# Second block's conditioning on one core: last layer's share moved into the first block's output, bias copies ahead of the latent attention, two recurrence weights on another queue

## The chip, the cores and the metric

The kernel runs on one core of a Trainium2 chip. The core has TensorE (PE, matrix products), VectorE (DVE), ScalarE (ACT), GpSimd (POOL) and SyncE (SP), which here only issues DMAs; ACT and POOL issue some as well. Each engine executes its own instructions in the order in which they stand. The metric is the device time of one execution in microseconds (us): a median of three runs, and beside it one profiled execution, from which all rows below come.

## The reference, cut to what matters

Two transformer blocks follow each other. The first has one hybrid layer: half of its width goes through a recurrence that is run in both directions, half through a latent attention (MLA). The second has four attention layers, and each needs a conditioning vector of 3072 numbers for the latent and one for the context.

```
# first block, one layer
mod = silu(c) @ ada_w + ada_b ;  h = rms_norm(x) * (1 + scale) + shift
w_log = -softplus(-(w0 + tanh(w_in) @ w2)) - 0.5 ; a = sigmoid(a0 + a_in @ a2)
rw = recurrence(forward) + recurrence(backward), group norm, gate
mla = softmax attention over latent and context, gate
x = rms_norm(x + gate * (concat(rw, mla) @ w_out)) * final_g
# second block, layers i = 0..3
sh, sc, gt    = split(silu(c) @ ada_w_2[i] + ada_b_2[i])
shc, scc, gtc = split(silu(c_ctx) @ ada_w_2[i] + ada_b_2[i])
h = rms_norm(x) * (1 + sc) + sh ; hc likewise
layer 1 alone: logits += rpb[head, row distance, column distance]
x = x + gt * ((attention(h, hc) * silu(z)) @ w_out)
```

The four conditionings of the second block depend on `c_2`, `c_ctx_2` and weights alone, so they can be worked out at any time before their layer.

## The kernel before, in words

The program is written stage by stage, and a scheduler then sets the order of the instructions on each engine, by the order of the program as priority and by when it thinks that an operand is there. The stages, by the profiled execution: the projections of the first block to about 155 us, the latent attention (`mla`) with the recurrence's inputs to about 457, the recurrence (`rwkv`, units prepared by `rw_prep`, solved by `rw_inv`, stepped by `rw_step`) to about 935, the output of the first block (`first`: per pair of token tiles a group norm `gnorm`, the product with `w_out`, the residual sum and the norm, and the preparation of layer 0) to about 1039, and the four layers of the second block to the end at 2976.

**Fillers.** The recurrence is a chain of small matmuls. Between them `rwkv` advances a generator, `fillers`, by the numbers in `fills`, and the generator issues two kinds of steps for the second block. One is the bias table of layer 1 (`rpb_rows`): the table is loaded, written flat to DRAM (`rpbf`), copied 16 times shifted (`rpbb`, 18 DMAs in all on SP), and then read back in eight steps, each with four matmuls (two instructions, two records each; L934) and a store. The other is the conditioning (`ada_wide`): a layer's `ada_w` is read in 24 tiles of 128x1024, 512 KB each (L277, SP's queue, two buffers named adw), and every tile is used by two matmul instructions that the trace shows as four records (L279). After each eight tiles VectorE adds the bias (L287) and two DMAs store the result `mods` (L288). Four layers are 96 tiles.

`rw_prep` begins with the decay: L1670 multiplies `wi` by `w2` (in the rows the tile is called w, as is `w0`), VectorE and ScalarE make `lw`, L1673 on POOL masks it, L1677 sums it along time, L1688 and L1692 do the same for `a`, and L1733 forms the products that `rw_inv` solves by blocks of 16 and 32 (L1826; its blocks are moved by the DMAs of L1796 to L1816 on SP). `first` loads the layer's context X45 (L1945), the gate `row` (L1952), and the residual X (L1962, from `xpart`), and adds the product to X on VectorE (L1974, L1975).

Of the kernel before, what the change touches and what calls it, by code (L numbers as in the profile page):

```python
# [317 lines left out]
class Block2(Kern):  # L318
# [10 lines left out]
    def run(self, ctx, xl, ctx_in, out, layers=4):  # L329
        if self.ps_ctx is None:  # L330
            self.psum(1, self.PS2)
        if self.mds is None:
            with self.tc.tile_pool(name="tmpa", bufs=1, reuse_waits="tile") as tp:
                sT = self.ada_cond(tp, self.a["c"], self.a["c_ctx"])
                self.mds = [self.ada(tp, sT, self.a["ada_w"][l], self.a["ada_b"][l], ("adw", 6)) for l in range(layers)]
                steps = self.rpb_rows(tp, self.a["b_rpb"][0], ("adw", 6))
                self.rpb = next(steps)
                for _ in steps:
                    pass
# [565 lines left out]
    def rpb_rows(self, sp, rpb, tag, ptag=None):  # L905
# [8 lines left out]
        nc.sync.dma_start(out=tab, in_=rpb.rearrange("h a b -> h (a b)"))  # L914
        nc.sync.dma_start(out=flat[64:7504].rearrange("(h n) -> h n", h=16), in_=tab)

        back = self.dr.tile([16, 128, 249], F32, name="rpbb")
        rows = self.dr.tile([16, 128, 249], F32, name="rpbr")
        yield rows
        for hf in range(2):  # L920
            for c in range(8):
# [3 lines left out]
                nc.sync.dma_start(out=back[:, 64 * hf + c:64 * hf + 64:8], in_=src)  # L925
# [214 lines left out]
class Block1(Block2):  # L1140
    second = None
    ebufs = 8
    fills = 1, 1, 2, 2, 1, 1
# [20 lines left out]
    def run1(self, x, ctx_in):  # L1164
# [8 lines left out]
        with ExitStack() as s0:  # L1173
# [16 lines left out]
            with ExitStack() as s1:  # L1190
# [29 lines left out]
                with tc.tile_pool(name="ap", bufs=1, reuse_waits="tile") as ap:  # L1220
# [3 lines left out]
                    self.md = self.ada(wp, sT, a["ada_w"][0], a["ada_b"][0], ("wr", self.wrbufs), None, None, range(2, 3))  # L1224
                    self.mla(W, q_d, kv_d, ap)
# [286 lines left out]
    def rwkv(self, rp, adp):  # L1512
# [15 lines left out]
        nc.sync.dma_start(out=self.w2, in_=a["rw_w2"][0].rearrange("d e f -> (d e) f"))  # L1528
        nc.sync.dma_start(out=self.a2, in_=a["rw_a2"][0].rearrange("d e f -> (d e) f"))
        nc.sync.dma_start(out=self.w0, in_=a["rw_w0"][0].unsqueeze(0).to_broadcast([128, 2, 512]))  # L1530
# [51 lines left out]
    def fillers(self, adp):  # L1582
# [4 lines left out]
        g = self.rpb_rows(adp, b["b_rpb"][0], ("adw2", 2), "ad")  # L1587
        self.rpb = next(g)
        yield from g
        for l in range(4):  # L1590
            g = self.ada_wide(adp, sT, b["ada_w"][l], b["ada_b"][l], ("adw", 3), "ad")
            self.mds.append(next(g))
            yield from g
# [342 lines left out]
    def first(self, sp, fx, xout, ctx_in):  # L1936
# [69 lines left out]

        self.gnorm(sp, 0)
        product(0)
        self.gnorm(sp, 1)
        if self.second:  # L2010
            self.prep(sp, self.by_token(X), ssq, *self.mods, False, (4, 5))
        rst = [norms(0)]
        product(1)
        rst.append(norms(1))
        for pair in range(2):
# [49 lines left out]
```

## Time and profile before

| | us |
|---|---|
| median of 3 runs (lowest, highest) | 2987.18 (2983.3, 3001.24) |
| the profiled execution | 2978.0 |
| its span | 2976.0 |
| PE busy | 2695.3 (91%) |
| DVE busy | 1787.2 (60%) |
| ACT busy | 1351.8 (45%) |
| POOL busy | 1248.4 (42%) |

The profiled execution lies 9 us below the median of the three runs. The mean granted clock of TensorE is 0.946 of full speed. Windows are stretches of the span in us from its start; a busy time in a window is that of the engine in it, and the count of instructions stands in brackets.

### The profile page before, as it was taken

Reading aid. Unit: us, or ns where it says so; the run is one execution under the profiler, and the core shown is the slowest. Engines: PE = TensorE matmul, PEld = TensorE weight load, DVE = VectorE, ACT = ScalarE, POOL = GpSimd, SP = SyncE. Lnnn points to the kernel's source line nnn. Section 1 sums busy time; section 2 is a strip of 40 time slices with the busy share of each in tenths; the row PEclk is TensorE's granted clock in tenths of the full one; section 3 lists DMA queues with packets and bytes.
Section 4 is the critical chain, followed back from the end, with each engine's and each line's share of the span. In section 5 each row is a group of like instructions: output and inputs, shape, how many; then the busy total and the mean of one; then the engine's idle time right before and its main releaser. Section 6 shows DMA issues by size and latency. Waiting matters only on the chain.

```text
span 2976.0 us, 55592 instructions
## 1 busy us (share of the span) xinstructions
PE 2695.3 (91%) x21935; PEld 2392.1 (80%) x21935; DVE 1787.2 (60%) x3409; ACT 1351.8 (45%) x2900; POOL 1248.4 (42%) x1328
## 2 busy tenths in 40 slices
PE   6989996899999499989989999997999998889999
PEld 4978885566668499978889899887988887788888
DVE  3344633677665636666455555546778686556675
ACT  3445631423323426556345445534545445345674
POOL 3214343264433543444534444663343244344444
PEclk8999995899995799999999999999999999999999
DMA  6143134555543211111221111322111121222112
GB/s 195 54 149 95 46 117 121 154 164 149 164 126 117 84 53 40 40 41 36 77 68 54 54 52 36 95 82 74 43 44 40 33 72 52 75 68 57 50 36 68
DMA packets 234591, 236.31 MB, mean 79 GB/s; under 512 B 57225, under 2 KB 210746, under 8 KB 234330
## 3 DMA queue, kind: packets, MB, share of 16 engines
q1 hardware_dynamic: 199616, 215.42, 24.6%
q10 hardware_dynamic: 33770, 16.29, 1.9%
q8 instruction: 172, 2.82, 0.4%
q0 software_dynamic: 944, 1.05, 0.2%
q14 instruction: 89, 0.73, 0.1%
HBM read 205.10 MB, written 28.07 MB: 78 GB/s over the span
## 4 chain that ended last, share of the span: by engine, by line
PE 66%; DVE 15%; DMA 6%; ACT 5%; issue 4%; POOL 2%; SPq 0%; ACTq 0%; DVEq 0%; POOLq 0%
PE psw L192 10%; PE psw L193 9%; PE psw L194 9%; PE psp L602 5%; PE ps L579 3%; PE psi L1826 2%; PE pad L279 2%; PE ps L580 2%; PE pso L594 2%; PE psw L1733 2%; PE psp L192 1%; PE psp L194 1%; PE psp L193 1%; DMA adw<-in_ada_w_dram 1%; DVE nm L562 1%
## 5 line engine op out<-in xcount | busy, mean ns | idle before, releaser
L185 POOL TENSOR_TENSOR wl<-wr,wh 128x512 fp32r<-128x512 f32 x362 | 477.9, 1336 | 593.7 <-ACT wh L408 482.3
L192 PE MATMUL psw<-wh,hh 128*128 128x256 f32 (+1 forms) x1888 | 546.0, 289 | 23.1 <-DVE pj L163 11.1
L194 PE MATMUL psw<-wh,hl 128*128 128x256 f32 (+1 forms) x1888 | 537.6, 285 | 1.8 <-POOL hl L185 1.8
L193 PE MATMUL psw<-wl,hh 128*128 128x256 f32 (+1 forms) x1888 | 536.6, 284 | 0.2 <-POOL wl L185 0.2
L192 PEld LDWEIGHTS psw<-wh,hh 128*128 128x128 f32 x1888 | 359.9, 191 | 33.6 <-DVE pj L163 13.6
L562 DVE TENSOR_REDUCE nm<-ps 128x1 f32<-128x768 f32 (+2 forms) x384 | 293.3, 774 | 152.0 <-PE ps L580 119.9
L194 PEld LDWEIGHTS psw<-wh,hl 128*128 128x128 f32 x1888 | 359.8, 191 | 2.8 <-POOL hl L185 2.4
L193 PEld LDWEIGHTS psw<-wl,hh 128*128 128x128 f32 x1888 | 360.2, 191 | 0.6 <-POOL wl L185 0.4
L408 ACT CAST wh<-wr 128x512 fp32r<-128x512 f32 x362 | 220.9, 617 | 248.0 <-PE psw L194 90.0
L563 ACT ACTIVATE P<-ps,nm 128x768 f32<-128x768 f32 (+1 forms) x288 | 246.8, 858 | 168.1 <-DVE nm L562 145.2
L570 DVE TENSOR_TENSOR ptl<-psp,pth 128x512 fp32r<-128x512 f32 x360 | 244.2, 686 | 128.8 <-ACT pth L569 126.4
L569 ACT CAST pth<-psp 128x512 fp32r<-128x512 f32 x360 | 207.3, 587 | 155.3 <-PE psp L602 126.0
L192 PE MATMUL psw<-hh,wh 128*128 128x512 f32 (+1 forms) x640 | 232.2, 363 | 23.2 <-DVE z L440 15.6
L193 PE MATMUL psw<-hl,wh 128*128 128x512 f32 (+1 forms) x640 | 226.5, 354 | 0.0
L194 PE MATMUL psw<-hh,wl 128*128 128x512 f32 (+1 forms) x640 | 226.3, 354 | 0.0
L579 PE MATMUL ps<-kh,qs 128*128 128x512 f32 (+1 forms) x608 | 203.1, 341 | 21.4 <-ACT P L563 14.1
L602 PE MATMUL psp<-ident,P 128*128 128x128 f32 x1408 | 218.8, 274 | 3.7 <-DVE P L1086 1.8
L580 PE MATMUL ps<-kz,qs 128*128 128x512 f32 (+1 forms) x608 | 183.4, 320 | 0.0
L602 PEld LDWEIGHTS psp<-ident,P 128*128 128x128 f32 x1408 | 164.7, 141 | 6.6 <-DVE P L1086 2.6
L192 PEld LDWEIGHTS psw<-hh,wh 128*128 128x128 f32 x640 | 122.8, 192 | 43.8 <-DVE z L440 19.7
L188 POOL TENSOR_SCALAR u<-ot 64x512 f32<-64x512 f32 x88 | 51.9, 590 | 250.8 <-ACT ot L620 247.4
L579 PEld LDWEIGHTS ps<-kh,qs 128*128 128x128 f32 x608 | 115.3, 190 | 38.8 <-ACT P L563 19.4
(509 smaller groups left out, 6645.1 us busy)
## 6 DMA issues: line engine op xcount, KB each, us to landing
adw<-in_ada_w_dram SPq DMA_DIRECT2D x96, 512.0 KB
wr<-in_a_w_in_dram SPq DMA_DIRECT2D x80, 256.0 KB
wr<-in_b_w_in_dram SPq DMA_DIRECT2D x64, 256.0 KB
wr<-in_c_w_in_dram SPq DMA_DIRECT2D x64, 256.0 KB
wr<-in_w_in_dram SPq DMA_DIRECT2D x52, 256.0 KB
adw<-in_ada_w_dram SPq DMA_DIRECT2D x48, 256.0 KB
xscr<-xt SPq DMA_DIRECT2D x36, 256.0 KB
wr<-in_a_w_out_dram SPq DMA_DIRECT2D x32, 256.0 KB
```

The lines of the kernel that those rows point to most:

```text
L185: self.nc.gpsimd.tensor_tensor(out=out, in0=in0, in1=in1, op=op)
L192: mm(out, lhsT=ah, rhs=bh, start=start, stop=False)
L193: mm(out, lhsT=ah, rhs=bl, start=False, stop=False)
L194: mm(out, lhsT=al, rhs=bh, start=False, stop=stop)
L408: nc.scalar.copy(out=h, in_=raw)
L562: nc.vector.tensor_reduce(out=nm, in_=S, axis=AX.X, op=ALU.max, negate=True)
L563: nc.scalar.activation(out=dst, in_=S, func=AF.Exp, bias=nm, accum_out=l)
L569: nc.scalar.copy(out=h[:, 0:n], in_=p[:, 0:n])
L570: nc.vector.tensor_tensor(out=lo[:, 0:n], in0=p[:, 0:n], in1=h[:, 0:n], op=ALU.subtract)
L579: mm(out[:, c0:c0 + n], lhsT=qs, rhs=kh[:, k0:k0 + n], start=True, stop=False)
L580: mm(out[:, c0:c0 + n], lhsT=qs, rhs=kl[:, k0:k0 + n], start=False, stop=True)
L602: self.nc.tensor.transpose(p[:, 256 * i + 128 * t:256 * i + 128 * t + 128], P[t][:, c0 + 128 * kt:c0 + 128 * kt + 128], self.ident)
```

## The change: what it does

Four edits. The making of the shifted bias copies becomes a function of its own (`rpb_back`), is called ahead of `mla`, and its 18 DMAs go to POOL's queue. `w2` and `w0` are loaded by ScalarE's queue, `a2` stays on SP's. The generator yields layer 0's conditioning first, then the eight bias steps, then layers 1 and 2; the 24 tiles of layer 3 are issued in `first`, in groups of 8, 4, 4, 4 and 4. All of `fills` are 1.

```diff
-    def rpb_rows(self, sp, rpb, tag, ptag=None):
+    def rpb_back(self, sp, rpb, tag):
...
-        nc.sync.dma_start(out=tab, in_=rpb.rearrange("h a b -> h (a b)"))
-        nc.sync.dma_start(out=flat[64:7504].rearrange("(h n) -> h n", h=16), in_=tab)
+        nc.gpsimd.dma_start(out=tab, in_=rpb.rearrange("h a b -> h (a b)"))
+        nc.gpsimd.dma_start(out=flat[64:7504].rearrange("(h n) -> h n", h=16), in_=tab)
...
-                nc.sync.dma_start(out=back[:, 64 * hf + c:64 * hf + 64:8], in_=src)
+                nc.gpsimd.dma_start(out=back[:, 64 * hf + c:64 * hf + 64:8], in_=src)
+        return back
...
-    fills = 1, 1, 2, 2, 1, 1
+    fills = 1, 1, 1, 1, 1, 1
...
+                    if self.second:
+                        self.back = self.rpb_back(ap, self.second["b_rpb"][0], ("th", 2))
                     self.mla(W, q_d, kv_d, ap)
...
-        nc.sync.dma_start(out=self.w2, in_=a["rw_w2"][0].rearrange("d e f -> (d e) f"))
+        nc.scalar.dma_start(out=self.w2, in_=a["rw_w2"][0].rearrange("d e f -> (d e) f"))
+        nc.scalar.dma_start(out=self.w0, in_=a["rw_w0"][0].unsqueeze(0).to_broadcast([128, 2, 512]))
         nc.sync.dma_start(out=self.a2, in_=a["rw_a2"][0].rearrange("d e f -> (d e) f"))
-        nc.sync.dma_start(out=self.w0, in_=a["rw_w0"][0].unsqueeze(0).to_broadcast([128, 2, 512]))
...
-        g = self.rpb_rows(adp, b["b_rpb"][0], ("adw2", 2), "ad")
-        self.rpb = next(g)
-        yield from g
-        for l in range(4):
+        rest = self.rpb_rows(adp, self.back, ("adw2", 2), "ad")
+        self.rpb = next(rest)
+        for l in range(3):
+            if l == 1:
+                yield from rest
             g = self.ada_wide(adp, sT, b["ada_w"][l], b["ada_b"][l], ("adw", 3), "ad")
...
+        fill = iter(())
+        if self.second:
+            b = self.second
+            sT = self.ada_cond(fx, b["c"], b["c_ctx"], "c1", True)
+            fill = self.ada_wide(fx, sT, b["ada_w"][3], b["ada_b"][3], ("adw2", 2), "c0")
+            self.mds.append(next(fill))
...
         self.gnorm(sp, 0)
+        some(8)
         product(0)
+        some(4)
         self.gnorm(sp, 1)
+        some(4)
         if self.second:
             self.prep(sp, self.by_token(X), ssq, *self.mods, False, (4, 5))
         rst = [norms(0)]
+        some(4)
         product(1)
         rst.append(norms(1))
+        some(4)
```

Three places of the new order matter. The first is SP's queue where the recurrence starts (`rpbb` are the shifted bias copies, the two `w` are `w2` and `w0`, `a` is `a2`, `xo` and `gb` belong to the stage before). Before:

```order
L925 DMA rpbb<-rpbf 16x8x249 x2
L1528 DMA w_4618<-in_rw_w_dram 128x512
L1529 DMA a_4619<-in_rw_a_dram 128x512
L1530 DMA w_4620<-in_rw_w_dram 128x1024
L925 DMA rpbb<-rpbf 16x8x249 x14
L931 DMA rpt<-rpbb 128x2x249 x2
```

And now:

```order
L277 DMA adw<-in_ada_w_dram 128x1024 x2
L1536 DMA a_4644<-in_rw_a_dram 128x512
L277 DMA adw<-in_ada_w_dram 128x1024 x6
L288 DMA mods<-ad_b_4733 2x512 x2
L277 DMA adw<-in_ada_w_dram 128x1024
L282 DMA ad_b_4917<-in_ada_b_dram 2x512 x2
L277 DMA adw<-in_ada_w_dram 128x1024 x7
L288 DMA mods<-ad_b_4917 2x512 x2
L282 DMA ad_b_5134<-in_ada_b_dram 2x512 x2
L277 DMA adw<-in_ada_w_dram 128x1024
L1803 DMA dd_4931<-dg 8x16x128
```

The bias copies are gone from SP, and the tiles of layer 0 stand in their place, two ahead of `a2` and the rest between it and the first DMA of the solve.

The second is TensorE at the same place, from the end of the stage before to the first products of the recurrence. Before:

```order
L206 MATMUL pad<-ident,ad_r 128x16
L1670 MATMUL psw<-w_4618,wi 128x512 x2
L1677 MATMUL psw<-tri,lw 128x128 x5
L1688 MATMUL psw<-ai,a_4619 128x128 x4
L1677 MATMUL psw<-tri,lw 128x128 x3
L934 MATMUL pad<-rpt,rpj 128x249 x2
L1692 MATMUL psw<-lt_65,sel 128x128 x4
L1688 MATMUL psw<-ai,a_4619 128x128 x4
L1692 MATMUL psw<-lt_65,sel 128x128 x4
L934 MATMUL pad<-rpt,rpj 128x249 x6
L1733 MATMUL psw<-x_4841,bk 128x64 x8
```

And now (L1677, L1684, L1695 and L1699 are L1670, L1677, L1688 and L1692 of before, seven lines further down):

```order
L206 MATMUL pad<-ident,ad_r 128x16
L279 MATMUL pad<-adw,ad_s 64x512 x8
L1677 MATMUL psw<-w_4643,wi 128x512 x2
L279 MATMUL pad<-adw,ad_s 64x512 x4
L1684 MATMUL psw<-tri,lw 128x128 x4
L279 MATMUL pad<-adw,ad_s 64x512 x2
L1684 MATMUL psw<-tri,lw 128x128
L1695 MATMUL psw<-ai,a_4644 128x128 x4
L1684 MATMUL psw<-tri,lw 128x128 x3
L279 MATMUL pad<-adw,ad_s 64x512 x2
L1699 MATMUL psw<-lt_65,sel 128x128 x4
L1695 MATMUL psw<-ai,a_4644 128x128 x4
```

Four tiles (eight instructions) stand ahead of the product with `w2` and ten more (twenty) between it and the first products L1733; no bias step is left there. All 24 tiles of layer 0 stand ahead of what ran at about 546 us, the eight bias steps where TensorE was from 546 to about 609, and 47 or 48 tiles from there to 822, where 58 were. From 822 to the end of the recurrence there are none, where 15 to 17 were.

The third is SP's queue in `first` (X45 is the context of layer 0, the first X after it the residual of the first pair, `zt` the gates of the recurrence's output, `row` the output gate and gain). Before:

```order
L1945 DMA X_9745<-in_ctx_dram 128x2x1024
L1952 DMA row_9756<-mods 128x1024
L1952 DMA row_9758<-in_final_g_dram 128x1024
L1608 DMA zt<-z_d 128x4x128 x2
L1962 DMA X_9852<-xpart 128x2x1024
L407 DMA wr<-in_w_out_dram 128x2x256 x3
L1962 DMA X_10249<-xpart 128x2x1024
```

And now:

```order
L407 DMA wr<-in_w_out_dram 128x2x256 x5
L1615 DMA zt<-z_d 128x4x128
L1952 DMA X_9624<-in_ctx_dram 128x2x1024
L1959 DMA row_9635<-mods 128x1024
L1959 DMA row_9637<-in_final_g_dram 128x1024
L200 DMA ad_r<-in_c_dram 8x128
L201 DMA ad_r<-in_c_ctx_dram 8x128
L277 DMA adw<-in_ada_w_dram 128x1024 x2
L282 DMA ad_b_9744<-in_ada_b_dram 2x512 x2
L1969 DMA X_9783<-xpart 128x2x1024
L1615 DMA zt<-z_d 128x4x128
L1969 DMA X_10238<-xpart 128x2x1024
```

X45, the rows and X, which stood ahead of the first `zt`, now stand behind the third of the four and behind eight loads of `w_out`; two tiles of layer 3 stand ahead of X.

## Rows read from the trace of the kernel before

**Rows 1.** Windows: length, busy (count) of PE, PEld, DVE, ACT, POOL, clock, DMA, GB/s.

```profile
457.00:546.00 89.00, 61.22 (x254) 43.71 (x254) 42.11 (x99) 24.68 (x58) 35.93 (x60) 0.61 0.47 128
546.00:610.00 64.00, 59.66 (x790) 41.52 (x790) 45.45 (x100) 24.39 (x66) 24.93 (x25) 0.85 0.58 154
610.00:822.00 212.00, 202.46 (x2622) 134.23 (x2618) 150.10 (x333) 64.05 (x169) 98.35 (x120) 0.98 0.56 155
822.00:889.00 67.00, 63.29 (x816) 43.34 (x814) 47.53 (x107) 17.16 (x46) 23.93 (x25) 0.90 0.47 138
889.00:935.00 46.00, 42.86 (x721) 40.31 (x719) 17.78 (x46) 14.22 (x41) 10.25 (x16) 0.57 0.45 137
960.00:1025.00 65.00, 34.54 (x312) 33.27 (x310) 51.42 (x102) 33.41 (x70) 39.80 (x25) 0.79 0.27 85
```

**Rows 2.** Same windows, L279 alone: PE busy (count), PEld, clock, DMA, GB/s.

```profile
457.00:546.00 89.00, 8.02 (x20) 1.32 (x20) 0.61 0.47 128
546.00:610.00 64.00, 20.90 (x66) 5.09 (x64) 0.85 0.58 154
610.00:822.00 212.00, 67.23 (x236) 12.62 (x232) 0.98 0.56 155
822.00:889.00 67.00, 20.20 (x70) 3.74 (x68) 0.90 0.47 138
```

**Rows 3.** Windows of 10 us, all engines, columns as in the first group.

```profile
810.00:820.00 10.00, 9.75 (x100) 7.62 (x99) 1.69 (x4) 4.12 (x11) 7.09 (x11) 1.00 0.70 160
910.00:920.00 10.00, 10.00 (x213) 9.88 (x213) 1.28 (x3) 1.81 (x5) 0.00 (x0) 0.50 0.80 268
```

**Rows 4.** Waits of PE from 457 to 940 us: total, count, longest, in us.

```profile
PE psw L1670 <- DMA w<-in_rw_w_dram: 9.3, 1, 9.3
PE pad L934 <- DMA rpt<-rpbb: 7.7, 4, 3.1
PE pad L279 <- DMA adw<-in_ada_w_dram: 7.0, 10, 2.0
PE psw L1677 <- POOL lw L1673: 5.3, 2, 4.7
```

**Rows 5.** L934 alone, window 457 to 546: PE busy, PEld, clock, share, GB/s.

```profile
457.00:546.00 89.00, 14.13 (x32) 8.48 (x32) 0.61 0.47 128
```

**Rows 6.** Timeline of SP's queue: start, duration, line, transfer, count.

```profile
464.30 9.89 SPq L925 DMA_DIRECT2D rpbb<-rpbf  x14
651.10 12.08 SPq L277 DMA_DIRECT2D adw<-in_ada_w_dram  x5
```

**Rows 7.** Timeline of POOL and PE: start, duration, instruction.

```profile
472.95 1.19 POOL L1673 TENSOR_SCALAR lw<-lw 128x512 f32<-128x512 f32 x2
545.99 3.68 PE L1733 MATMUL psw<-x,bk 128*128 128x64 f32 x16
```

**Rows 8.** Lines, 600 to 830 us: count | busy, mean ns | idle before.

```profile
L279 PE MATMUL pad<-adw,ad_s 128*64 128x512 f32 x248 | 72.2, 648 | 3.1 <-issue 1.7 <-DMA adw<-in_ada_w_dram 1.4
L1901 PE MATMUL psc<-R,x 128*128 128x64 f32 x144 | 18.8, 279 | 0.2 <-DVE R L1921 0.2
```

**Rows 9.** Lines, 889 to 935 us.

```profile
L1901 PE MATMUL psc<-R,x 128*128 128x64 f32 x48 | 9.3, 375 | 2.4 <-DVE y L1931 2.4
```

**Rows 10.** Timeline in the first block's output: SP's queue, then DVE.

```profile
903.00 0.41 SPq L1945 DMA_DIRECT2D X<-in_ctx_dram  x1
956.68 3.22 SPq L1608 DMA_DIRECT2D zt<-z_d  x2
...
962.46 1.15 DVE L1975 TENSOR_TENSOR X<-X,yt 128x512 f32<-128x512 f32 x1
```

**Rows 11.** Forms of a line: count, then shortest/median/longest ns, first and last start.

```profile
L287 DVE TENSOR_TENSOR ad_b<-pad,ad_b x24: 666/684/689, 560.7 to 891.0; 2x512 f32<-2x512 f32 x24
...
L116 POOL DMA_DIRECT2D sel<-in_const_dram x5: 592/612/737, 1.3 to 2577.1; - x5
```

**Rows 12.** Chain that ended last: a landing of a tile, start, duration.

```profile
611.88 4.95 DMA adw<-in_ada_w_dram
```

More of the change, by code (lines that the diff above doesn't have):

```diff
@@ L335, in run @@
                 self.mds = [self.ada(tp, sT, self.a["ada_w"][l], self.a["ada_b"][l], ("adw", 6)) for l in range(layers)]
-                steps = self.rpb_rows(tp, self.a["b_rpb"][0], ("adw", 6))
+                steps = self.rpb_rows(tp, self.rpb_back(tp, self.a["b_rpb"][0], ("adw", 6)), ("adw", 6))
                 self.rpb = next(steps)
@@ L913, in rpb_rows @@
         tab = sp.tile([128, 512], F32, tag=tag[0], bufs=tag[1], name="rpt")[0:16, 0:465]
-        nc.sync.dma_start(out=tab, in_=rpb.rearrange("h a b -> h (a b)"))
-        nc.sync.dma_start(out=flat[64:7504].rearrange("(h n) -> h n", h=16), in_=tab)
+        nc.gpsimd.dma_start(out=tab, in_=rpb.rearrange("h a b -> h (a b)"))
+        nc.gpsimd.dma_start(out=flat[64:7504].rearrange("(h n) -> h n", h=16), in_=tab)
         back = self.dr.tile([16, 128, 249], F32, name="rpbb")
-        rows = self.dr.tile([16, 128, 249], F32, name="rpbr")
-        yield rows
         for hf in range(2):
@@ L924, in rpb_rows @@
                 src = bass.AP(tensor=src.tensor, offset=src.offset, ap=[[465, 16], [31, 8], [1, 249]])
-                nc.sync.dma_start(out=back[:, 64 * hf + c:64 * hf + 64:8], in_=src)
+                nc.gpsimd.dma_start(out=back[:, 64 * hf + c:64 * hf + 64:8], in_=src)
+        return back
+    def rpb_rows(self, sp, back, tag, ptag=None):
+        nc = self.nc
+        rows = self.dr.tile([16, 128, 249], F32, name="rpbr")
+        yield rows
         J = sp.tile([128, 128], F32, tag="rpj", bufs=1, name="rpj")
@@ L2005, in store, with some @@
             nc.sync.dma_start(out=xout.rearrange("(t p) n -> p t n", p=128)[:, tiles[0]:tiles[1] + 1:tiles[1] - tiles[0]], in_=x)
+        fill = iter(())
[4 more added lines that the diff above has]
+            self.mds.append(next(fill))
+        def some(n):
+            for _ in range(n):
+                next(fill, None)
         self.gnorm(sp, 0)
+        some(8)
         product(0)
+        some(4)
         self.gnorm(sp, 1)
+        some(4)
         if self.second:
```

## The prediction, made before the changed kernel was run

> **What bounds the kernel now.** I read the windows by stage first. From 457 to 935 us, the recurrence, TensorE is busy 61.2 of 89, 59.7 of 64, 202.5 of 212, 63.3 of 67 and 42.9 of 46 us, and no other engine is above 75% in any of these [rows 1]. After the start, then, the stage is as long as TensorE's own work, and what is taken off TensorE counts unless a wait fills the hole. The start is different: 28 of its 89 us TensorE is idle. The first block's output is different again: from 960 to 1025 VectorE has 51.4 of 65 us and TensorE 34.5 [rows 1].
>
> Then the share of the conditioning in it. L279 takes 8.0, 20.9, 67.2 and 20.2 us of the first four windows [rows 2]. A tile is four records: 248 records are 62 tiles in 72.2 us, so 1.16 us each [rows 8].
>
> Then the clock. At 810 to 820 us, tiles running, it is 1.00 (2.4 GHz); at 910 to 920, the last tile gone since 889, it is 0.50 (1.2 GHz), though TensorE is busy all of the 10 us [rows 3]. The long matmuls of the tiles go with the high level, and the small ones of the recurrence, alone, with the low one. The same step L1901 takes 279 ns among tiles and 375 ns without [rows 8, 9], a factor of 1.34.
>
> Last the waits at the start: 9.3 us for `w2`, 7.7 us in four waits for the bias copies, 7.0 us in ten waits for tiles, 5.3 us for POOL's `lw` [rows 4].
>
> **The change, term by term**, against the profiled 2978.0 us, which lies 9 us under the median of 2987.
>
> 1. *457 to 546.* Gone: the wait for `w2` (9.3), the waits for bias copies (7.7) and the bias matmuls (14.1, [rows 5]), 31.1 us. New: 24 tiles. With two buffers five of them were issued in 12.08 us [rows 6], 2.4 us each, so 24 need 58 us, beside 61.2 - 14.1 - 8.0 = 39 us of TensorE's other work. Two things do not move. L1677 needs what POOL masks at 472.95 [rows 7], so of the wait for `w2` only what lies ahead of that is gained. And the solve's first DMA now stands on SP behind some 20 tiles, 48 us by the same rate; TensorE in its order waits with every late tile. The stage ended with the L1733 at 545.99 [rows 7]. Best end: 31.1 less the 11 us by which 58 + 39 exceed 89 less 3, or -20. Worst: tiles that are late as now and no gain, +5. I take -5, near the worst, since 58 us of loads begin only when the buffers of the stage before are free.
>    ScalarE's queue makes no transfer faster here: what the wait of 9.3 us holds is the place behind bias copies, of which 14 take 9.89 us to issue [rows 6]. The Trainium skill says as much ("Trainium Kernel Development and Optimization", Key Constraints): queues of several engines end on the same 16 DMA engines and save issue time only. By that a load that is already running beside `w2` slows it on any queue, and less than the 9.3 would go; the -5 stands without it.
> 2. *546 to 610.* Out: 20.9 us of tiles [rows 2]. In: the eight bias steps, 14.1 us at a clock of 0.61 [rows 5], about 8 at full clock. The other 59.7 - 20.9 = 38.8 us of TensorE ran at a mean of 0.85, about 70% of them at the high level; without tiles they go to the low one, 0.34 x 0.7 x 38.8 = +9. That is -4 to +2, and a round trip per bias step can add the 7.7 us of waits. I take 0; bounds -12 (clock stays) to +15.
>    The Trainium skill ("TensorE: Matmul & The Clock Gate", Part 1) has a rule against the +9: the throttled state is the default, and a busy TensorE is released to 2.4 GHz. By it this term would be -12 and term 4 -20. The window at 910 us, busy all along at 0.50, does not agree with it.
> 3. *610 to 822.* 59 tiles (236 records, [rows 2]) become 48 by the order: 11 x 1.16 = -12.8. Some of them stood in waits of the chain; I take -9, bounds -13 to 0.
> 4. *822 to 889.* 17 tiles, 20.2 us, go out [rows 2]. The other 43.1 us of TensorE fall from 0.90 to the low level: 0.34 x 0.8 x 43.1 = +11.7. So -8; VectorE, 47.5 of 67 us here [rows 1], holds the chain, so I take -6, bounds -20 to 0.
> 5. *889 to 935.* No tiles before or after, low clock already (0.57, [rows 1]): 0.
> 6. *The first block's output.* X and its row were asked for from 903.00 on, 53 us ahead of the later `zt` at 956.68 [rows 10]. Now they stand behind a `zt` of that kind, and ahead of the end of X go X45 (1 MB), two rows (1 MB), two tiles (1 MB) and X itself (1 MB). At the 268 GB/s of [rows 3], 4 MB are 15.6 us: X is there at about 956.7 + 15.6 + 2 = 974, where VectorE adds to it at 962.46 [rows 10]. That is 12 us late; VectorE has other work of about 5 us that the new order puts ahead. +7, in the stretch that VectorE bounds. Its new work, six L287 of 0.684 us [rows 11], is 4.1 us, half of it in gaps: +2. TensorE's 24 tiles, 28 us at 1.16, lie in its idle 30 of 65 us. Sum +9, bounds 0 to +18.
> 7. *POOL.* 18 issues at 0.612 us [rows 11] are 11 us on an engine that is busy 42% of the span by the table, early in the latent attention; what could be hurt is a POOL step that is waited for there. Such an issue with 128 rows does not occur on POOL before. +1, bounds 0 to +8.
>
> The second block's layers keep their order and get 0. Sum: -5 + 0 - 9 - 6 + 0 + 9 + 1 = **-10**, that is 2968 profiled, and 9 more for the median: **2977**.
>
> **Rivals.**
>
> *The clock stays high without tiles.* Terms 2 and 4 become -12 and -20 and term 3 -13: -5 - 12 - 13 - 20 + 9 + 1 = -40, 2947. For it: the fall at 889 has one example, and the matmuls of 546 to 822 come from several units at once, so more densely than those of the tail. Against: the 10 us at 910 are as dense as can be, and at 0.50 [rows 3]. This is also the time by the skill's rule above. 0.22.
>
> *The 24 tiles bound the first block's output.* Every tile's load has its place on SP between loads of `w_out` and of layer 0's weights, which wait for POOL to free their buffers, and every tile's matmul has its place on TensorE ahead of the product's or the layer's. Two buffers hide one tile. If they come one by one at the 4.95 us of a landing in the chain [rows 12], 24 take 119 us from about 972, so the stage ends at 1091 and not at 1039: +52. With -20 from terms 1 to 4, 0 from term 6's other parts and +1: +33, so 2978 + 33 + 9 = 3020. From 2.8 us per tile on ((1039 - 972) / 24) the stage grows; above 3.6 us ((1039 + 20 - 972) / 24) the change is a loss. For it: 4.95 us is what a landing takes when a tile is waited for. Against: 2.4 us per tile in the recurrence with the same two buffers [rows 6]. 0.18.
>
> *The fillers were hidden.* If the recurrence is as long as its solves on VectorE and its small DMAs, TensorE's busy time is only spread, and taking tiles out gives nothing: 0 for terms 1 to 4, +10 for the rest, 2997. For it: VectorE is at 71% in 546 to 889. Against: TensorE at 95% there [rows 1]. 0.10.
>
> **How the numbers follow.** Forecast 0.50, rivals 0.22, 0.18 and 0.10. What a measurement of this kernel can tell from no change is about 1%, 30 us: faster is under 2957, slower above 3017. The forecast's own bounds (-30 to +25 about it, by the terms' ends, which do not all fall together) are almost all inside. The first rival is faster in nearly all of its cases, 0.20, and 0.03 come from the forecast's lower end. The second is slower in about two thirds of its cases, 0.13, and 0.02 come from the forecast's upper end. Same: 0.62. The range reaches down to the first rival with a few us (2943) and up to the milder cases of the second (3012).
>
> **What would show it.** Right: the first L1677 still near 473 after POOL; tiles dense from 460 to 530; a granted clock near 0.5 from 822 to 935 and lower than 0.85 from 546 to 610; L1901 near 375 ns there; the recurrence 15 to 25 us shorter; X's addition 5 to 10 us later in `first`, and the stage 5 to 15 us longer. Wrong: the clock at 1.00 past 822 (first rival), waits of 2 us and more for every tile in `first` and TensorE idle before layer 0 (second), the recurrence at its 478 us (third), or latent attention longer by over 8 us through POOL's copies.

## The result, and the profile after

The changed kernel takes 3012.11 us (median of 12 runs, 2993.07 to 3024.63), the kernel before in the same session 2993.62 us (12 runs). The ratio is 1.0065 with a 95% interval of 1.0047 to 1.0083: slower, by 19 us. The forecast was 10 us faster. The profiled execution has a span of 2995.1 us against 2976.0, so the two traces differ by the same 19 us and can be laid side by side, instruction by instruction.

The windows of the changed kernel, with the stretches and columns of [rows 1]:

```profile
457.00:546.00 89.00, 67.82 (x318) 34.26 (x316) 41.62 (x92) 16.22 (x38) 29.75 (x50) 0.77 0.54 167
546.00:610.00 64.00, 55.16 (x665) 48.28 (x664) 38.30 (x90) 24.27 (x61) 18.36 (x19) 0.68 0.26 63
610.00:822.00 212.00, 201.67 (x2635) 138.61 (x2633) 159.23 (x344) 70.32 (x184) 106.64 (x127) 0.92 0.48 133
822.00:889.00 67.00, 63.72 (x900) 55.08 (x899) 47.54 (x111) 21.61 (x59) 30.42 (x36) 0.77 0.12 21
889.00:935.00 46.00, 35.24 (x623) 33.92 (x623) 16.75 (x45) 12.03 (x33) 7.71 (x11) 0.52 0.19 46
960.00:1025.00 65.00, 52.64 (x360) 34.97 (x359) 49.18 (x95) 32.03 (x69) 30.98 (x23) 0.84 0.75 251
```

In these two traces the clock went where the tiles went: up at the start (0.77 for 0.61), down where the bias steps now stand (0.68 for 0.85) and from 822 on. TensorE is as busy from 610 to 889 as before, with fewer tiles. In the last window TensorE's load has gone from 34.5 to 52.6 us.

The waits of TensorE from 457 to 940 us (total, count, longest), which answer to [rows 4]:

```profile
PE pad L279 <- DMA adw<-in_ada_w_dram: 17.6, 15, 4.8
PE pad L938 <- DVE ad_b L287: 3.8, 1, 3.8
PE pad L279 <- issue: 3.0, 1, 3.0
```

The wait for `w2` and the four for the bias copies, 17.0 us, are gone, and TensorE now waits 17.6 us for tiles, 10.6 more than the 7.0 before. The timeline of TensorE at the start shows where (the idle time before an instruction and what ended it stand in brackets):

```profile
465.72 3.68 PE L279 MATMUL pad<-adw,ad_s 128*64 128x512 f32 x8 [3.04 <-issue]
474.22 3.68 PE L279 MATMUL pad<-adw,ad_s 128*64 128x512 f32 x8 [4.81 <-DMA adw<-in_ada_w_dram]
477.83 1.25 PE L1677 MATMUL psw<-w,wi 64*128 64x512 f32 x4
```

The product with `w2` (L1677 now) waits for nothing of its own and yet begins at 477.83, where it began at 466.81: it stands behind four tiles. The recurrence itself began 5.2 us later (the transposition L206 at 462.45 for 457.27), so 5.8 us of the 11 arose here. Nor did the load of `w2` come much earlier in the stage. ScalarE's queue has it behind six stores of the stage before:

```profile
450.19 16.95 ACTq L1480 DMA_DIRECT2D xpart<-xo  x6
467.23 0.42 ACTq L1534 DMA_DIRECT2D w<-in_rw_w_dram  x1
```

That is 4.8 us after the transposition. Before, on SP's queue, it was issued 5.5 us after it:

```profile
462.76 0.53 SPq L1528 DMA_DIRECT2D w<-in_rw_w_dram  x1
```

So even without the four tiles the product could not have begun much sooner than before.

Those 5.2 us come from the attention. POOL there, first before, then now (start, duration, instruction):

```profile
186.32 0.10 POOL L1286 MEMSET up<- 128x1 f32 x1 [0.53 <-DVE kT L1292]
```

```profile
186.79 4.79 POOL L922 DMA_DIRECT2D rpbb<-rpbf  x9
194.46 2.71 POOL L922 DMA_DIRECT2D rpbb<-rpbf  x5 [2.88 <-DMA rpbb<-rpbf]
197.16 0.12 POOL L1292 MEMSET up<- 128x1 f32 x1
```

And VectorE's step that needs that tile, before and now:

```profile
195.12 0.75 DVE L1291 SCALAR_TENSOR_TENSOR kT<-up,ccol,kT 128x512 f32<-128x512 f32 x1 [0.78 <-ACT kT L1290]
```

```profile
201.97 0.74 DVE L1297 SCALAR_TENSOR_TENSOR kT<-up,ccol,kT 128x512 f32<-128x512 f32 x1
```

A memset of 0.1 us stands behind fourteen copies on POOL, the tenth of which waits 2.88 us for an earlier one to land. The memset is 10.8 us late, its slack was 8.8 us before the step needed it, and with VectorE's order the step is 6.9 us late; VectorE's instructions between 300 and 400 us are 6.7 us later.

At the end of the first block's output, TensorE (the idle time in brackets):

```profile
1049.00 1.08 PE L279 MATMUL pad<-adw,ad_s 128*64 128x512 f32 x4 [2.81 <-DMA adw<-in_ada_w_dram]
1051.46 1.92 PE L279 MATMUL pad<-adw,ad_s 128*64 128x512 f32 x4 [1.38 <-DMA adw<-in_ada_w_dram]
1053.31 0.58 PE L192 MATMUL ps<-wh,hh 128*128 128x256 f32 x1
```

Layer 0 begins right behind the last tile, at 1053.31 where it began at 1038.64. TensorE alone (busy, clock, share and rate of the DMA) from the last step of the recurrence to layer 0, before and now, and its largest wait in the second:

```profile
955.50:1038.60 83.10, 45.61 (x388) 0.77 0.25 82
955.90:1053.30 97.40, 74.92 (x466) 0.83 0.73 243
```

```profile
PE pad L279 <- DMA adw<-in_ada_w_dram: 18.5, 9, 5.1
```

TensorE has 29.3 us more work there, and its idle time fell only from 37.5 to 22.5 us, since 18.5 us of what is left are waits for the tiles themselves. The difference of the two is the 14.3 us by which the stretch is longer.

X came late as predicted. First its load on SP's queue, then its addition on VectorE:

```profile
956.12 0.50 SPq L1952 DMA_DIRECT2D X<-in_ctx_dram  x1
```

```profile
971.04 1.78 DVE L1982 TENSOR_TENSOR X<-X,yt 128x512 f32<-128x512 f32 x1
```

The addition is 8.6 us later than in [rows 10], though the last step of the recurrence ends at the same time in both traces (955.5 and 955.9).

### The profile page after: what moved, and what is told of

It is laid out like the page before. It is cut to its first block, busy times and chain, and to the rows that moved or that the text cites. A ratio compares the mean times of both kernels' runs of the same rounds, so it can differ in the third digit from the quotient of the medians.

```text
span 2995.1 us, 55597 instructions
## 1 busy us (share of the span) xinstructions
PE 2721.7 (91%) x21936; PEld 2399.8 (80%) x21936; DVE 1793.9 (60%) x3412; ACT 1354.0 (45%) x2901; POOL 1254.2 (42%) x1346
## 4 chain that ended last, share of the span: by engine, by line
PE 67%; DVE 16%; DMA 5%; ACT 4%; issue 4%; POOL 3%; SPq 0%; ACTq 0%; DVEq 0%; POOLq 0%
PE psw L192 10%; PE psw L193 9%; PE psw L194 9%; PE psp L602 5%; PE psi L1833 3%; PE ps L579 3%; PE pad L279 3%; PE ps L580 2%; DMA adw<-in_ada_w_dram 2%; PE pso L594 2%; PE psw L1740 2%; PE psp L192 1%; PE psp L194 1%; PE psp L193 1%; PE psp L683 1%
## 5 line engine op out<-in xcount | busy, mean ns | idle before, releaser
L185 POOL TENSOR_TENSOR wl<-wr,wh 128x512 fp32r<-128x512 f32 x362 | 471.2, 1317 | 604.6 <-ACT wh L408 488.4
L192 PE MATMUL psw<-wh,hh 128*128 128x256 f32 (+1 forms) x1888 | 544.6, 288 | 22.5 <-DVE pj L163 10.5
L279 PE MATMUL pad<-adw,ad_s 128*64 128x512 f32 x384 | 132.5, 765 | 39.2 <-DMA adw<-in_ada_w_dram 36.1
```

The source lines that it names most:

```text
L185: self.nc.gpsimd.tensor_tensor(out=out, in0=in0, in1=in1, op=op)
L192: mm(out, lhsT=ah, rhs=bh, start=start, stop=False)
L279: nc.tensor.matmul(p[64 * j:64 * j + 64], lhsT=sT[:, k], rhs=wt[:, 512 * j:512 * j + 512], start=(k == 0), stop=(k == 7), tile_position=(0 ...
```

## The experiments

Ratios are to the kernel before, run on the same chip in the same session. The table gives lengths by the traces: the recurrence from the transposition L206 to the end of its last step (L1924), the third unit's product with `w2` from that start, and the output from the last step to the memset L1053 that stands beside layer 0's first matmul. One traced execution each. How far two executions differ is shown by e1: its TensorE has the instructions of the recurrence in the very order of before, its ratio is 0.9999, and yet its recurrence is 12.6 us longer in the trace. So a recurrence that differs by some 13 us shows nothing by itself. The output is steadier: 81.6 to 83.2 us in the eight kernels that keep both tiles and bias steps out of it, e3 apart, and 98.5 to 102.1 in the seven that load 24 tiles there.

| kernel | recurrence | third unit | output | ratio |
|---|---|---|---|---|
| before, 96 tiles | 498.2 | 114 | 83.0 | 1 |
| e1: before, w2 and w0 on ScalarE's queue | 510.8 | 124 | 83.1 | 0.9999 |
| the change | 493.5 | 132 | 99.0 | 1.0065 |
| e8: the change, copies on SP | 513.7 | 131 | 102.0 | 1.0034 |
| e4: the change without layer 3 | 503.4 | 129 | 82.7 | 1.0019 |
| e5: before with 72 tiles | 484.8 | 116 | 83.1 | 0.9924 |
| e6: before with no tile | 457.9 | 119 | 81.6 | 0.9867 |
| b1: before, layer 3 in the output | 487.2 | 117 | 98.5 | 1.0019 |
| b2: b1 with a pool of its own | 478.8 | 114 | 98.5 | 1.0000 |
| c1: b1 with layer 0 first | 507.6 | 124 | 99.5 | 1.0079 |
| b3: 8 tiles in the output | 495.6 | 110 | 88.8 | 0.9988 |
| d1: bias steps in the output | 514.0 | 120 | 85.4 | 1.0011 |

### The single edits: w2 and w0 (e1), the copies (e2, e8)

```diff
-        nc.sync.dma_start(out=self.w2, ...
+        nc.scalar.dma_start(out=self.w2, ...
```

> Kernel before with one edit: w2 and w0 are loaded by ScalarE's queue. Theory A (the wait for w2 was real, but the next thing is late soon after: L1677 waits for POOL's lw near 473 us): the wait of 9.3 us at the first product with w2 falls to under 4 us, and the kernel gains 3 to 6 us (ratio 0.998 to 0.999). Theory B (the start of the recurrence is set by the bias steps and the solve, whose places on SP do not change): the wait goes and the time stays within 1 us.

Measured: 0.9999 (0.9977 to 1.0022). The time is theory B's, but the wait, which both theories let go, stays:

```profile
PE psw L1670 <- DMA w<-in_rw_w_dram: 7.5, 1, 7.5
```

The load is issued at 458.97, again behind six stores on ScalarE's queue and 3.0 us after the transposition (5.5 before), and the product comes 7.7 us after it (9.5 before). So the place behind the bias copies was not what the wait of 9.3 us held; the order above has `w2` behind two of them and ahead of the other fourteen. The Trainium skill ("Trainium Kernel Development and Optimization", Key Constraints) would let a second queue save issue time only; the run agrees, since no more than 1.8 us of the wait went. The window from 546 to 610 of this trace (TensorE alone) shows that the clock, too, differs between two executions of one order, 0.71 here and 0.85 in [rows 1]:

```profile
546.00:610.00 64.00, 60.31 (x709) 0.71 0.47 125
```

```diff
+                        self.back = self.rpb_back(ap, self.second["b_rpb"][0], ("th", 2))
                     self.mla(W, q_d, kv_d, ap)
```

> Kernel before with one edit: the 18 DMAs of the bias copies are issued by POOL ahead of the latent attention; fillers, fills, w2, w0 and the first block's output as before. Theory A (the memsets of up stand behind 14 copies on POOL and delay VectorE's kT): +6 to +8 us in the attention by 300 us of the span, -3 to -8 at the start of the recurrence, where the bias steps no longer wait for the copies; sum -2 to +5 us. Theory B (the 7 us in the attention of the changed kernel come from the granted clock there and not from POOL): 0 to 1 us in the attention, and the whole -3 to -8.

Measured: 1.0136 (1.01 to 1.0173), 41 us slower, far outside both. The attention is 9.8 us later from 300 to 400 us of the span, somewhat more than theory A's 6 to 8. The rest is the recurrence, 531.1 us. The bias steps no longer wait for copies, and four tiles stand ahead of the second unit and fourteen more ahead of the third, where before had none and ten. That this order is the cause is not shown: a1 below has the same eighteen tiles there, 24 tiles fewer later on, and a recurrence of 491.0.

```diff
-                nc.gpsimd.dma_start(out=back[:, 64 * hf + c:64 * hf + 64:8], in_=src)
+                nc.sync.dma_start(out=back[:, 64 * hf + c:64 * hf + 64:8], in_=src)
```

> Changed kernel with the 18 DMAs of the bias copies at the same place of the program, ahead of the latent attention, but on SP's queue and not on POOL's. Theory A (on POOL they stand ahead of the memsets of up, and VectorE's kT waits for those): the attention is back at before's time within 2 us at 300 us of the span, and the kernel 5 to 8 us faster than the changed one. Theory B (the copies' traffic or the granted clock costs the 7 us): no faster than the changed kernel.

Measured: 1.0034 (1.0013 to 1.0054), against the change's 1.0065 some 9 us faster, with intervals that overlap. The attention shows it plainly: the recurrence begins at 458.4 us (457.3 before, 462.4 with the change), and the step on VectorE is back:

```profile
196.73 0.75 DVE L1297 SCALAR_TENSOR_TENSOR kT<-up,ccol,kT 128x512 f32<-128x512 f32 x1 [0.77 <-ACT kT L1296]
```

Theory A. What cost in the attention was the queue on which the copies stand, not their place or their 2 MB. The recurrence of this trace, 513.7 us, is not read: its execution lies 11 us above the median of this kernel's runs.

### What a tile is worth in the recurrence (e5, e6, e7, b5)

```diff
         for l in range(4):
+            if l == 3:
+                self.mds.append(self.mds[2])
+                continue
```

> Kernel before with 72 of the 96 tiles in the recurrence: layer 3's conditioning is left out, and layer 3 uses layer 2's vector. It gives what taking 24 tiles out of the recurrence is worth with nothing put elsewhere. Theory A (without tiles between them the small matmuls run at the low clock, so the tiles' time is given back): recurrence 488 to 503 us by the profile where it was 498, ratio 0.997 to 1.001, mean granted clock of the recurrence lower than 0.83. Theory B (the prediction's: TensorE's busy time bounds the stage and the clock takes only part back): 15 to 28 us faster, ratio 0.990 to 0.995.

Measured: 0.9924 (0.9899 to 0.9949), 23 us faster. Theory B: the last 24 tiles cost about 0.95 us each, an estimate from the ratio.

> Kernel before with no tile at all: the second block's conditioning is left out, its vectors are copies of the bias ada_b. Theory A: the 96 tiles were 111 us of TensorE at 1.16 us each, but the recurrence without them is 30 to 60 us shorter at most, with L1901 near 375 ns and a granted clock near 0.5 to 0.6 throughout. Theory B: 90 to 115 us shorter.

Its edit puts a copy of `ada_b` in the place of the loop over the layers. Measured: 0.9867 (0.9842 to 0.9893), 40 us faster, and the recurrence 40 us shorter: theory A on the time. With e5, the other 72 tiles are worth 17 us by these two ratios, about a quarter of a microsecond each. The windows of the recurrence, before and without tiles, and L1901 (its line is 1902 here) from 600 to 830 us without tiles:

```profile
457.00:955.00 498.00, 444.33 (x5347) 316.89 (x5349) 320.94 (x714) 149.72 (x391) 205.87 (x251) 0.83 0.51 143
```

```profile
457.00:912.00 455.00, 369.78 (x4959) 330.23 (x4960) 304.96 (x684) 149.47 (x391) 204.39 (x251) 0.68 0.18 44
```

```profile
L1902 PE MATMUL psc<-R,x 128*128 128x64 f32 x160 | 27.6, 350 | 4.9 <-DVE R L1922 3.3 <-DVE y L1930 1.6
```

L279 alone in the first of these windows:

```profile
457.00:955.00 498.00, 116.91 (x384) 22.77 (x384) 0.83 0.51 143
```

Tiles were 116.9 us of TensorE's 444. Without them it is busy 370, not 327: the rest grew by 42 us, the clock fell from 0.83 to 0.68, and the step that took 279 ns among tiles [rows 8] takes 350. But the clock is not at the low level throughout, as theory A has it. Two windows of this run without any tile, TensorE alone:

```profile
610.00:620.00 10.00, 10.00 (x185) 0.50 0.01 3
630.00:640.00 10.00, 10.00 (x182) 1.00 0.01 2
```

TensorE is busy all the time in both, with matmuls of at most 128 columns, and the first has the low level (1.2 GHz) and the second the high one (2.4 GHz). So the prediction's reading of [rows 3], that the small matmuls of the recurrence alone go with the low level, is too simple. The Trainium skill's rule that activity releases the clock ("TensorE: Matmul & The Clock Gate", Part 1) agrees with the second window, but the first window and the one at 910 us in [rows 3] are as busy and were granted 0.50. What decides between the levels stays open.

> Kernel before, where each layer's 24 tiles are multiplied from one loaded tile: 92 of the 96 loads of 512 KB are left out, all matmuls are kept. Theory A (the loads are hidden; what counts is TensorE's order and clock): within 8 us of before. Theory B (the loads hold up the solve's small DMAs and the tiles' own matmuls): 10 to 30 us faster.

The edit loads a tile once per layer. Measured: 1.006 (1.0041 to 1.0079), slower, against both. The scheduler, which no longer sees loads, puts 20 and 32 tiles into the second and third unit instead of 10 and 23, and the recurrence is 512.9 us. So the run does not price the loads by themselves: with them the order changed, and the new order cost more than leaving out the loads gave.

```diff
-    fills = 1, 1, 2, 2, 1, 1
+    fills = 1, 2, 3, 3, 1, 1
```

> Kernel before with one edit: fills 1, 2, 3, 3, 1, 1 instead of 1, 1, 2, 2, 1, 1, so that the 96 tiles are spent earlier. Theory A (tiles in the last third cost 0.8 us each and earlier ones 0.2 to 0.4): no tile after 820 us of the span, 5 to 12 us faster, ratio 0.996 to 0.998. Theory B (more tiles between two solve steps delay the chain as much as they save at the end): 0.999 to 1.003.

Measured: 1.004 (1.002 to 1.0061), slower and nearer to theory B, but the tiles hardly moved: the tiles per unit are those of before within one, and 18 still come after 820 us. It decides nothing on early tiles.

### Layer 3 in the output (e3, e4, b1, b2, f1, b3)

> Changed kernel without layer 3's conditioning: its 24 tiles, their matmuls and stores are left out, and layer 3 uses layer 2's vector. It gives the price of the 24 tiles where the change puts them. Theory A (the tiles themselves, their traffic and their places in TensorE's order make the 15 us): 13 to 17 us faster than the changed kernel, and the first matmul of layer 0 comes within 93 to 96 us of the last step of the recurrence. Theory B (X and its row are late because the order puts them behind the gates and w_out, tiles or not): 3 to 7 us faster only, with the first addition to X still near 971 us.

Measured: 1.0019 (0.9998 to 1.004), 14 us faster than the change, with an output as long as before's: theory A.

> Changed kernel with layer 3's 24 tiles given back to the recurrence (after layers 1 and 2), nothing of it in the first block's output. Theory A (late X and tiles that TensorE waits for cost 15 us in the first block's output, and the recurrence gained only 8 us by losing 24 tiles): 5 to 10 us faster than the changed kernel, 9 to 14 us slower than before. Theory B (24 tiles are 28 us of TensorE, which bounds the recurrence): as slow as the changed kernel or up to 13 us slower than it.

The edit is `range(4)` in the fillers and no tile in the output. Measured: 1.0092 (1.006 to 1.0125), theory B. The last 14 tiles come after 889 us. The output is long again (98.4 us) without a tile in it, because the transposes of the first group norm begin 14.4 us after the last step, a wait of TensorE for VectorE, where before they began ahead of it. Why VectorE comes to them so late is not shown.

```diff
-        for l in range(4):
+        for l in range(3):
...
+            fill = self.ada_wide(fx, sT, b["ada_w"][3], b["ada_b"][3], ("adw2", 2), "c0")
```

> Kernel before with one edit: layer 3's 24 tiles leave the recurrence for the first block's output, as the change does it; the order of the other fillers, fills, copies, w2 and w0 stay. From the run with 72 tiles (24 tiles less in the recurrence: 0.9924) and the changed kernel against its version without layer 3 (1.0065 against 1.0019: 24 tiles in the output cost about 14 us): theory A, the two add up: -23 + 14 = -9 us, ratio 0.996 to 0.999. Theory B (what the recurrence gains is lost again in the output): 1.000 to 1.004.

Measured: 1.0019 (0.9994 to 1.0045), theory B: 11 us shorter in the recurrence, 15.5 longer in the output.

```diff
-            sT = self.ada_cond(fx, b["c"], b["c_ctx"], "c1", True)
+            fy = self.tc.tile_pool(name="fy", bufs=1, reuse_waits="tile")
+            fp = fy.__enter__()
+            sT = self.ada_cond(fp, b["c"], b["c_ctx"], "c1", True)
```

> The kernel b1 with one edit more: the buffers of layer 3's tiles and of its vector come from a memory pool of their own, opened after X45, the rows and X, and not from the pool of X45, the rows and X. In the order of SP these loads then stand ahead of the first gates again, as before. Theory A (X and its row are late because their memory is free later in the larger pool): the first addition to X comes 8 us earlier, and the kernel is 4 to 9 us faster than b1, ratio to before 0.993 to 0.996. Theory B (the tiles themselves bound the output): within 2 us of b1.

Measured: 1.0000 (0.9978 to 1.0023), on time between the two theories. X is on time again, 8 us after the last step (936.7) and not 15, but layer 0 does not begin earlier for it:

```profile
944.86 1.16 DVE L1975 TENSOR_TENSOR X<-X,yt 128x512 f32<-128x512 f32 x1
```

```profile
1033.93 0.58 PE L192 MATMUL ps<-wh,hh 128*128 128x256 f32 x1 [3.61 <-DVE htmp L687]
```

The output is 98.5 us as in b1. So the pool did make X late, and X's lateness was not the price: the output is theory B's.

> Changed kernel, where the 24 tiles in the first block's output are multiplied from one loaded tile: 23 loads of 512 KB are left out there, all matmuls are kept. Theory A (the loads come too slowly beside w_out, X and layer 0's weights, and TensorE waits for them in its order): the output is 84 to 90 us long where it was 99, 8 to 14 us faster than the changed kernel, ratio to before 1.002 to 1.004. Theory B (the matmuls' own time on TensorE at the low clock, or VectorE's additions): within 4 us of the changed kernel.

The edit loads one tile for all 24 in the output. Measured: 1.0056 (1.0033 to 1.0078), output 94.5 us, nearer to theory B. TensorE's waits for tile loads go, and these are now its longest (before has the first one too, 11.7 us ahead of the same step):

```profile
PE psw L684 <- issue: 12.1, 1, 12.1
PE pad L280 <- DVE ad_b L288: 7.7, 2, 6.5
```

The output is 4.5 us shorter than the change's 99.0. That is not the price of the loads by itself, for without them the scheduler puts 22 of the 24 tiles ahead of the second group norm's transposes, where the change has six. How the 16 us divide between the loads and the tiles' place in TensorE's order stays open.

> Kernel before with one edit: the last 8 tiles of layer 3 alone go into the first block's output, after its first group norm, from a pool of their own; 88 tiles stay in the recurrence. Theory A (a tile at the end of the recurrence costs about 0.8 us, and TensorE's idle 18 us before the second group norm hides 8): recurrence 490 to 493 us, output 83 to 86, ratio to before 0.997 to 0.999. Theory B (tiles in the output cost as much as in the recurrence): 0.999 to 1.002.

Measured: 0.9988 (0.9969 to 1.0007), no difference that these runs can tell from none. Output 88.8, so 0.7 us per tile, not clearly less than the 0.95 us of a late tile in the recurrence (e5).

### The order of the fillers (c1, a1, a2, d1)

```diff
-        yield from g
         for l in range(3):
+            if l == 1:
+                yield from rest
```

> The kernel b1 (before, layer 3's tiles in the first block's output) with one edit more: layer 0's tiles stand ahead of the bias steps. The copies stay on SP at the start of the recurrence. Theory A (24 tiles instead of 10 ahead of the third unit's preparation, which TensorE executes in order, make the recurrence of the changed kernel longer): that preparation begins near 130 us of the recurrence and not near 116, recurrence 5 to 12 us longer than b1's 487, ratio to before 1.003 to 1.006. Theory B (the copies' place does it): as b1, 1.001 to 1.003.

Measured: 1.0079 (1.005 to 1.0107), 18 us slower than b1, recurrence 20 us longer. The third unit's product with `w2` comes 7 us later than in b1, its L1733 26 us later (637 for 611). From 580 to 625 us, where b1 has tiles and c1 bias steps, first b1, then c1:

```profile
580.00:625.00 45.00, 38.54 (x636) 26.41 (x633) 33.62 (x75) 16.74 (x47) 26.54 (x30) 0.96 0.58 175
```

```profile
580.00:625.00 45.00, 40.87 (x560) 31.59 (x559) 27.56 (x61) 21.54 (x56) 21.00 (x26) 0.78 0.34 87
```

TensorE is busier in c1 and does fewer matmuls, though of another mix, 560 for 636: the clock is 0.78 for 0.96. The price that theory A names is there and larger than it says; that the tiles ahead make it is not shown by this run alone, since the bias steps in the middle may do their part.

> Changed kernel with one edit: the eight bias steps stand ahead of layer 0's tiles again. Theory A (layer 0's tiles stand ahead of the product with w2 and take the place of the wait that was removed): that product comes 4 to 6 us earlier, the third unit's preparation 10 us earlier, and the kernel is 5 to 15 us faster than the changed one, ratio to before 1.001 to 1.005. Theory B (the order at the start does not matter, since the solve sets the pace): within 3 us of the changed kernel.

Measured: 1.0054 (1.003 to 1.0079), within the change's interval: theory B on time. The product with `w2` came 5 us earlier and the third unit stayed at 130, with 18 tiles still ahead of it. So with the copies made early the order of the fillers, which cost 18 us in c1, is worth nothing that these runs can tell.

> Changed kernel with one edit: fills 1, 1, 2, 2, 1, 1 as before, so that the tiles are spent earlier. Theory A (tiles in the last third of the recurrence, where TensorE is the bound, cost their time; those earlier cost a quarter of it): no tile after 800 us of the span, recurrence 8 to 12 us shorter, ratio to before 1.002 to 1.004. Theory B (fills do not matter): within 3 us of the changed kernel, 1.006 to 1.007.

Measured: 1.0084 (1.0054 to 1.0114), theory B. No tile after 800 us, and the recurrence is no shorter (496.9).

```diff
-        yield from g
+        self.back = self.rpb_back(adp, b["b_rpb"][0], ("adw2", 2))
...
         product(0)
+        some(5)
```

> Kernel before with two edits: the eight bias steps leave the recurrence and stand in the first block's output, with a pool of their own, after the first product and before the second; w2 and w0 on ScalarE's queue, which alone changed nothing. The copies stay on SP at the start of the recurrence, and all 96 tiles in the recurrence, from its start. Theory A (bias matmuls in the middle of the recurrence let the clock fall, tiles do not; 14 us of bias matmuls fit into TensorE's idle time in the output): recurrence 485 to 495 us with the third unit's preparation near 116 to 122, output 83 to 88, ratio to before 0.994 to 0.998. Theory B (24 tiles ahead of the third unit are what makes the recurrence longer, wherever the bias steps stand): third unit near 130, recurrence 500 to 508, ratio 1.002 to 1.006.

Measured: 1.0011 (0.9989 to 1.0033), the same as before, and neither theory. The bias steps do fit into the output (85.4 us), and the third unit comes at 120. The recurrence of this trace is 514.0 us, and its third solve begins at 259 us, where before's began at 220 and e1's at 226; but by the ratio the kernel is at most 10 us slower than before, so part of this belongs to the one execution. With 27 tiles ahead of the third unit and no bias step in the recurrence d1 keeps before's time, and c1, with 24 tiles ahead and the bias steps in the middle, does not. Over all kernels the tiles ahead of the third unit do not order the recurrences: e2, e7, c1 and d1 have 18 to 27 and are over 505 us, but the change has 24 and 493.5, and e1 has before's 10 and 510.8. What in the order makes a recurrence long stays open.

No version that computes all of the conditioning beats the kernel before beyond its interval. The intervals of b1, b2, b3 and d1 lie below the changed kernel's.

## Why the prediction was wrong, by its own steps

Shifts between the two traces, matched instruction by instruction (one execution each, so a line's figure carries the spread that e1 shows):

| stretch | terms | forecast | measured |
|---|---|---|---|
| latent attention, to 457 us | 7 | +1 | +5.2 |
| 457 to 546 us | 1 | -5 | +5.4 |
| 546 to 602 us | 2 | 0 | +3.4 |
| 602 to 955 us | 3, 4, 5 | -15 | -13.6 |
| first block's output, to layer 0 | 6 | +9 | +14.3 |
| second block | none | 0 | +4.4 |
| sum | | -10 | +19.1 |

The boundary at 546 us is the L1733 at 545.99 of [rows 7], in the changed kernel:

```profile
556.56 3.52 PE L1740 MATMUL psw<-x,bk 128*128 128x64 f32 x16
```

The boundary at 602 us is a step of the recurrence that both have, L1907 in the trace before and L1914 now:

```profile
602.61 0.48 PE L1907 MATMUL psc<-R,x 128*64 128x64 f32 x2 [2.31 <-DVE R L1921]
```

```profile
616.60 0.64 PE L1914 MATMUL psc<-R,x 128*64 128x64 f32 x8
```

**Term 1, the start, is the step that failed.** It was forecast at -5 and measured +5.4, just above its worst end, and has 10 of the 29 us of the miss. One pair of traces would not show this, since e1, with before's order, is itself 9.0 us late at the boundary at 602. But the other kernels agree. The L1733 at 545.99 comes 84.1 to 88.8 us after the transposition in the seven that begin the recurrence as before does (before, e1, e5, b1, b2, b3, b5), and 90.8 to 97.6 us in the six that begin it as the change does (the change, e3, e4, e8, f1, a2).

Term 1 took the wait for `w2`, 9.3 us, as gone because the load left SP's queue. It did not go: on ScalarE's queue the load stands behind six stores, and in e1, where this is the only edit, 7.5 us of the wait are left. In its place the prediction's other sentence came true, "TensorE in its order waits with every late tile", which it had charged only as the worst end. The product with `w2` stands behind four tiles, 15.4 us after the transposition and not 9.5, and TensorE's waits for tiles grew by 10.6 us, 10.4 of them in this stretch. The sign named for a right forecast, the first L1677 still near 473, failed with it: that product (L1684 now) begins at 483.17.

**Term 2** measured +3.4 against 0, inside its bounds. The clock fell as it had counted, to 0.68; but e1 has 0.71 in this window with the order of before, so this fall does not show the rule behind the term.

**Terms 3 to 5** measured -13.6 against -15, closer than a single trace can tell. From the boundary at 602 to the last step it is 339.3, 338.5 and 351.2 us in the change, f1 and e4, and 352.9, 356.4 and 362.4 in before, e1 and b5, so the sign holds in every pair and the size is in part luck. The reason given, fewer tiles with the clock taking a part back, fits, though the clock from 822 to 889 was 0.77 and not at the low level that term 4 counted with. e5 and e6 bear out that tiles late in the recurrence cost nearly their time and the others little.

**Term 6 had the wrong mechanism and, by it, too small a size.** X came late by about the predicted amount, and b2 shows that this was not what the stage waited for. What failed is the sentence that TensorE's 24 tiles, 28 us, lie in its idle time: TensorE's work grew by 29.3 us, 18.5 us of its idle time went to waits for the tiles, and only 15 us of idle time were filled. This is the second rival in its mild form: at 2.8 us per tile it was to begin, and (1053.31 - 972.16) / 24 = 3.4 us per tile were measured, the last tile just ahead of layer 0. Eight tiles alone do no better per tile, 0.7 us each (b3), than the 24.

**Term 7 was mis-sized inside its bounds** (0 to +8), +5.2 against +1; e8 shows the cause. The row of the memset's slack, 8.8 us, was not set against fourteen copies of 0.53 us and a wait of 2.88 between them.

**The second block's 4.4 us need not be from the change.** All but 339 of TensorE's 13507 records there stand in the same place, and the kernels of the experiments, none of which edits it, have 1934 to 1948 us there, before 1937.4 and the change 1940.2 (from L1053 on).

Two single removals account for the slowdown by their ratios: the copies off POOL's queue give 9 us (e8), layer 3's tiles out of the output 14 us (e4), together 23 of the 19, each with an interval of several us. The recurrence, in which the forecast saw its gain of 20 us, gave none that these runs can tell.

Of the rivals, a clock that stays high without tiles is refuted by e6 as a mean (0.68 with no tile), though some stretches there are at 1.00. Hidden fillers are refuted by e5 for the last 24 tiles, and came near the truth for the other 72 (17 us for 72 x 1.16 = 84 us of TensorE). The tiles as the bound of the output came true in part.

## What to carry to other kernels

On an engine that executes in order, a wait that is removed is worth what the next instruction in the order allows: read which instructions now stand there, and charge their own waits. A load that changes its queue has a place in the new queue too; read what stands ahead of it there before you book the wait as gone. Filler work has a price that depends on its place, here 0.25 us to 0.95 us for the same tile of 1.16 us, so moving it to an idle stretch gains only the difference of the two prices. And a queue that is idle for long is not free: look for the 0.1 us instruction behind what is put on it, and for its slack. Before a stretch of two traces is compared, look how far it differs between two executions of one order.

## What the runs showed of the hardware

With 96 tiles among its small matmuls the mean granted clock of the recurrence is 0.83, with none 0.68, and taking out 117 us of matmuls gave back only 40 us. Without any tile, 10 us in which TensorE was busy throughout were granted 0.50 in one place and 1.00 in another (e6). One order of instructions had a clock of 0.85 in one execution and 0.71 in the other from 546 to 610 us, and a recurrence of 498.2 and 510.8 us (before, e1). Fourteen copies of 128 pieces each took POOL 10.4 us to issue, with a stop of 2.88 us after the ninth; on SP fourteen took 9.89 us [rows 6].
